# Three groups of stores issued from ScalarE's queue in place of GpSimd's, in a one-core decoder layer

## The chip, the cores and the metric

The kernel runs on one core of one Trainium2 chip. The metric is the device time of one execution in microseconds (us), as the median of the runs shown. Engines are named as in the profile: PE (TensorE matmul), PEld (its weight loads), DVE (VectorE), ACT (ScalarE), POOL (GpSimd), SP (SyncE, which here only issues transfers). A store or a load is issued by the queue of one of these engines and then carried out by the core's 16 DMA engines.

## The reference

One layer over a sequence of 1024 tokens with 1024 channels in float32: four token mixers behind one combined projection, an output projection, a LayerNorm on the residual, then a SwiGLU channel mixer of width 2816 and a second LayerNorm.

```python
h = x * (1 + sc1) + sh1
z = h @ w_in + b_in                       # split into seven groups of 256 channels
y = concat([y_a, y_b, y_c, y_d])          # short conv, pooling, conformer conv (31 taps), state space
x = layer_norm(ALPHA * x + (1 + g1) * (y @ w_o), ln1_g, ln1_b)
h = x * (1 + sc2) + sh2
f = (silu(h @ w_gate) * (h @ w_up)) @ w_down
x = layer_norm(ALPHA * x + (1 + g2) * f, ln2_g, ln2_b)
```

## The kernel before

**Products.** Every large product is done in three passes (`passes`, L130 to L132): each float32 operand is split into a high part, cast by ACT (L80), and the rest, subtracted by DVE (L81). A weight tile is therefore usable when its L80 and its L81 are done; the first matmul that needs the L81 part is the third, L132.

**Halves.** The tokens go in two halves `c` of 512 (`CH`). Half 0 passes the output projection and the first LayerNorm around 255 to 305 us of the span, half 1 around 372 to 460 us.

**The first LayerNorm** works on tiles of 128 tokens, four in a half. `res1` (DVE, L570 and L571) forms the row `r`, `norm_stats` takes its mean and variance (DVE, L500 and L503) and the reciprocal root in ten tiny instructions on POOL (`rsqrt`, L397 to L415, then `lnb` at L578). ACT normalises `r` (L580). The first store keeps it in DRAM as `x1_d` (L581). PE transposes `r` (L588), ACT scales the turned row (L598, eight pieces) into a buffer `tmp`, both parts are split off, and the second store keeps the turned row as `h2_d` (L603). In half 1, DVE subtracts two loaded blocks from it (L609), POOL stores the difference (`t1_d`, L613), and ACT and DVE cast the results into `tb`.

**The gate and up products** of a pair of 128-column blocks `j` (`c11`): `gu_pairs` loads and splits two weight tiles, `c11_mm` computes one block product, ACT keeps a copy of it in `p1` (L643) before PE adds the second one on top, and `c11_act` stores `p1` in DRAM (`p1_d`, L646, the third store of the change), applies SiLU (ACT, L648), multiplies (DVE, L649) and stores the result (`act_d`, L650, POOL). `c11` of the pairs 0 and 1 is interleaved with the LayerNorm of half 0; pairs 2 to 6 run between the halves, beside the 31-tap convolution of half 1 on DVE (L429, "taps") and the conformer norm that follows the taps (`conformer`); later pairs run beside the LayerNorm of half 1. From about 514 us on, seven-product blocks (`strassen`) and the down projection fill PE.

**Order.** PE's order is fixed by hand throughout (`in_order`), and in the stage with the LayerNorm of half 0 the orders of DVE and ACT too. Elsewhere a scheduler sets DVE's, ACT's, POOL's and SP's order from its own estimates when the program is built, so an edit on one queue can move instructions on others. Each engine works through its list strictly in order. Weight loads, all `raw` tiles (four buffers, `p1` among them) and the loads that read the stores back are on SP's queue.

Of the kernel before, what the change touches and what calls it, by code (L numbers as in the profile page):

```python
# [16 lines left out]
P = 128  # L17
# [3 lines left out]
CH = 512  # L21
# [29 lines left out]
def trunk(ctx: ExitStack, tc: tile.TileContext, A, out):  # L51
    nc = tc.nc
    V, S, G, PE, SP = nc.vector, nc.scalar, nc.gpsimd, nc.tensor, nc.sync
# [11 lines left out]
    def mm():  # L65
        return ps.tile([P, 512], F32, name="mm", tag="mm", bufs=6)
# [9 lines left out]
    def tmp(cols=1024):  # L76
        return sl.tile([P, cols], F32, name="tmp", tag="tmp", bufs=3)

    def split(hi, lo, src):
        S.copy(hi, src)  # L80
        V.tensor_tensor(out=lo, in0=src, in1=hi.bitcast(F32), op=SUB)  # L81
# [136 lines left out]
    for i in range(4):  # L218
        r = slice((i % 2) * 64, (i % 2) * 64 + 64)
# [128 lines left out]
    for i in range(2):  # L348
        for hf in range(2):
            w = 2 << (2 * i + hf)  # L350
            r = slice(64 * hf, 64 * hf + 64)
# [133 lines left out]
    x1_d = dr.tile([T // P, P, D], F32, name="x1_d")  # L485
    h2_d = dr.tile([KT, P, T], F32, name="h2_d")
    t1_d = dr.tile([KT // 2, P, CH], F32, name="t1_d")
    p1_d = dr.tile([FT // 2, P, 2, CH], F32, name="p1_d")
# [3 lines left out]
    def norm_stats(r, res=None):  # L492

        st = cst.tile([P, 2, 6], F32, name="lst", bufs=2)
        mv = cst.tile([P, 2], F32, name="lmv", bufs=2)
        rs = cst.tile([P, 1], F32, name="lrs", bufs=2)
        for h in range(2):
            if res:
                run(res, 1)
            V.bn_stats(st[:, h], r[:, h * 512:(h + 1) * 512])  # L500
            if res and h == 0:
                yield
        V.bn_aggr(mv, st)  # L503
        rsqrt(rs, mv[:, 1:2])
        return rs, mv[:, 0:1]
# [68 lines left out]
    def ln1(c, t, r, h2):  # L574

        rs, nm = yield from norm_stats(r)
        nb = cst.tile([P, 1], F32, name="lnb", bufs=2)
        G.tensor_scalar(out=nb, in0=nm, scalar1=rs, scalar2=-1.0, op0=MUL, op1=MUL)  # L578
        yield
        S.activation(r, r, AF.Identity, scale=rs, bias=nb)  # L580
        G.dma_start(x1_d[c * 4 + t], r)  # L581
        yield
        tp = []
        for h in range(2):
            o = mm()
            for k in range(4):
                kk = 4 * h + k
                PE.transpose(o[:, k * P:(k + 1) * P], r[:, kk * P:(kk + 1) * P], ident)  # L588
            tp.append(o)
        yield  # L590
        ht = tmp()
        hv = ht.rearrange("p (k t) -> p k t", k=KT)
        tt = slice(t * P, (t + 1) * P)
        for h in range(2):
            for k in range(4):
                kk = 4 * h + k
                src, dst = tp[h][:, k * P:(k + 1) * P], ht[:, kk * P:(kk + 1) * P]
                S.activation(dst, src, AF.Identity, scale=hA[:, kk:kk + 1], bias=hB[:, kk:kk + 1])  # L598
            if c == 0:
                ks = slice(4 * h, 4 * h + 4)  # L600
                split(h2[:, ks, 0, tt], h2[:, ks, 1, tt], hv[:, ks])
                yield
        G.dma_start(h2_d[:, :, c * CH + t * P:c * CH + (t + 1) * P].rearrange("k p t -> p k t"), hv)  # L603
        if c == 1:

            b11 = raw_p.tile([P, 1024], F32, name="raw", tag="raw", bufs=4)
            bv = b11[:, :CH].rearrange("p (k t) -> p k t", k=4)
            SP.dma_start(bv, h2_d[:4, :, t * P:(t + 1) * P].rearrange("k p t -> p k t"))
            V.tensor_tensor(out=bv, in0=hv[:, :4], in1=bv, op=SUB)  # L609
            split(tb[0][:, :4, 0, tt], tb[0][:, :4, 1, tt], bv)  # L610
            split(tb[1][:, :, 0, tt], tb[1][:, :, 1, tt], hv[:, 5:])
            split(tb[0][:, 4, 0, tt], tb[0][:, 4, 1, tt], hv[:, 4])
            G.dma_start(t1_d[:, :, tt].rearrange("k p t -> p k t"), bv)  # L613
# [29 lines left out]
                S.copy(p1[:, i * CH + lo:i * CH + lo + n], z[i][:, hs])  # L643

    def c11_act(j, z, p1):
        G.dma_start(p1_d[j].rearrange("p a t -> p (a t)"), p1)  # L646
        g = tmp()
        S.activation(g[:, :CH], z[0], AF.Silu)  # L648
        V.tensor_tensor(out=g[:, :CH], in0=g[:, :CH], in1=z[1], op=MUL)  # L649
        G.dma_start(act_d[2 * j][:, :CH], g[:, :CH])  # L650

    def p1_tile():
        return raw_p.tile([P, 1024], F32, name="p1", tag="raw", bufs=4)

    def c11(j, tiles=(None, None)):

        w = gu_pairs(j, tiles)
        yield
        z, p1 = [mm(), mm()], p1_tile()
        c11_mm(w, z, p1, 0)  # L660
        yield
        c11_mm(w, z, p1, 1)
        c11_act(j, z, p1)
# [204 lines left out]
    with in_order(ON_PE):  # L868
# [53 lines left out]
        def stats(t):  # L922
            rr.append(res1(0, t, o0))
            ln.append(ln1(0, t, rr[t], h2))
            run(ln[t], 1)
# [3 lines left out]
    with in_order(ON_PE, ON_DVE, ON_ACT):  # L929
# [16 lines left out]
        wg.append(pair(raw(A["w_up"][0])))  # L946
        run(ln[2], 1)
        ln.append(ln1(0, 3, rr[3], h2))
        run(ln[3], 1)
        B["11"] = [(h2[:, k, 0], h2[:, k, 1]) for k in range(4)]  # L950
        B["21"] = [(h2[:, k, 0], h2[:, k, 1]) for k in range(4, 8)]
        z, p1 = [mm(), mm()], p1_tile()
# [13 lines left out]
        for q in range(2):  # L966
            c11_mm(w1, z1, p11, q, 256, 256)
        c11_act(0, z, p1)
        c11_act(1, z1, p11)
    ln_end = [[i for i in nc.cur_bb.bb.instructions if i.engine == e][-3]  # L970
              for e in (ON_DVE, ON_ACT)]
    fins = []
    with tc.issue_after(ln_end[0]), tc.issue_after(ln_end[1]), in_order(ON_PE):
# [19 lines left out]
        def done(t, o):  # L993
            rr.append(res1(1, t, o))
            ln.append(ln1(1, t, rr[t], None))
            run(ln[t], 1)
# [429 lines left out]
```

## Time and profile before

| | before |
|---|---|
| runs, us | 1037.73, 1038.14, 1041.8 |
| median, us | 1038.14 |
| the profiled execution's own time, us | 1037.87 |
| its span (first to last instruction), us | 1036.1 |
| PE busy, share of the span | 95% |
| DVE, ACT, POOL busy | 71%, 33%, 18% |

The profile is of one execution: 1.8 us of its time lie outside the span. Times of day in the text are us from the span's start. PE's matmuls overlap, so a row's length is longer than its step in the stream.

### The profile page before, as it was taken

The numbers are of one execution on the slowest core, as the hardware profiler recorded it, in microseconds if no ns is written. First come the engines' busy times: TensorE is split into PE (matmuls) and PEld (weight loads), VectorE is DVE, ScalarE is ACT, GpSimd is POOL, SyncE is SP. The second block draws the span as 40 slices with busy tenths as digits, with TensorE's granted clock in tenths as the row PEclk, the third lists the DMA queues.
The fourth block names the chain that finished last, engine by engine and source line by source line (L and its number), as shares of the span: only waits on it lengthen the run. The fifth ranks groups of instructions, "written<-read, shape, count | busy, mean of one in ns | idle before, by whom it ended". The sixth has DMA issues, their size and how long they took to land.

```text
span 1036.1 us, 12527 instructions
## 1 busy us (share of the span) xinstructions
PE 980.8 (95%) x4480; PEld 799.9 (77%) x4480; DVE 737.7 (71%) x1184; ACT 344.5 (33%) x537; POOL 184.4 (18%) x515
## 2 busy tenths in 40 slices
PE   8949999898989989899899999999999999999995
PEld 7837777676887868687688888887888888888884
DVE  5858998888669952757898777776568433776656
ACT  4632211424464351374322222222233333312500
POOL 7990000300351020541000000000000000050013
PEclk9979999998999999899999999999999999999998
DMA  8833212686454363597954344443247534654601
GB/s 314 321 112 104 53 41 90 219 225 223 158 204 172 147 237 104 188 316 267 347 175 159 138 147 152 146 148 111 82 149 284 174 136 142 232 185 148 228 21 61
DMA packets 65694, 177.75 MB, mean 172 GB/s; under 512 B 11040, under 2 KB 17216, under 8 KB 65632
## 3 DMA queue, kind: packets, MB, share of 16 engines
q1 hardware_dynamic: 57760, 149.17, 42.7%
q0 software_dynamic: 7872, 27.79, 6.7%
q8 instruction: 35, 0.57, 0.2%
q14 instruction: 27, 0.22, 0.1%
HBM read 142.26 MB, written 34.09 MB: 170 GB/s over the span
## 4 chain that ended last, share of the span: by engine, by line
PE 60%; DVE 10%; DMA 5%; POOL 4%; ACT 3%; issue 2%; SPq 0%; DVEq 0%; POOLq 0%; ACTq 0%
PE mm L132 18%; PE mm L130 18%; PE mm L131 17%; PE sm L130 2%; PE sm L132 2%; PE sm L131 2%; DMA raw<-in_w_ada_dram 2%; DMA raw<-h_d 2%; DVE pr L81 1%; DVE acc L429 1%; DMA raw<-in_w_gate_dram 1%; DVE raw L168 1%; ACT tmp L598 1%; DVE lst L500 1%; POOL rs_a L397 1%
## 5 line engine op out<-in xcount | busy, mean ns | idle before, releaser
L81 DVE TENSOR_TENSOR pr<-raw,pr 128x1024 fp32r<-128x1024 f32 (+1 forms) x139 | 138.1, 1003 | 77.7 <-ACT pr L80 77.4
L80 ACT CAST pr<-raw 128x1024 fp32r<-128x1024 f32 (+1 forms) x139 | 119.2, 878 | 179.4 <-PE sm L132 68.4
L130 PE MATMUL mm<-bop,pr 128*128 128x512 f32 x264 | 103.2, 391 | 4.2 <-DVE c L767 3.5
L131 PE MATMUL mm<-bop,pr 128*128 128x512 f32 x264 | 102.8, 389 | 0.0
L132 PE MATMUL mm<-bop,pr 128*128 128x512 f32 x264 | 102.7, 389 | 0.0
L130 PE MATMUL mm<-h,pr 128*128 128x512 f32 (+1 forms) x208 | 77.0, 370 | 8.0 <-ACT p L643 7.1
L429 DVE SCALAR_TENSOR_TENSOR acc<-up,pack,acc 128x512 f32<-128x512 f32 x120 | 84.3, 742 | 0.1
L130 PE MATMUL mm<-pr,acts 128*128 128x512 f32 x216 | 84.0, 389 | 0.0
L131 PE MATMUL mm<-pr,acts 128*128 128x512 f32 x216 | 84.0, 389 | 0.0
L132 PE MATMUL mm<-pr,acts 128*128 128x512 f32 x216 | 84.0, 389 | 0.0
L132 PE MATMUL mm<-h,pr 128*128 128x512 f32 (+1 forms) x208 | 75.4, 362 | 2.9 <-DVE pr L81 2.9
L131 PE MATMUL mm<-h,pr 128*128 128x512 f32 (+1 forms) x208 | 75.2, 361 | 0.0
L132 PE MATMUL mm<-tb,pr 128*128 128x512 f32 x176 | 68.8, 391 | 1.1 <-DVE pr L81 1.0
L130 PE MATMUL mm<-tb,pr 128*128 128x512 f32 x176 | 68.7, 390 | 1.0 <-ACT pr L80 1.0
L131 PE MATMUL mm<-tb,pr 128*128 128x512 f32 x176 | 68.5, 389 | 0.0
L397 POOL TENSOR_SCALAR rs_a<-lmv 128x1 f32<-128x1 f32 x16 | 11.0, 689 | 318.1 <-DVE lmv L503 317.8
L168 DVE SCALAR_TENSOR_TENSOR raw<-raw,cond 128x1024 f32<-128x1024 f32 x48 | 58.1, 1218 | 13.3 <-DMA raw<-in_w_ada_dram 13.2
L80 ACT CAST pr<-room 128x512 fp32r<-128x512 f32 x60 | 34.3, 619 | 87.9 <-PE mm L132 83.9
L130 PEld LDWEIGHTS mm<-bop,pr 128*128 128x128 f32 x264 | 49.6, 188 | 16.4 <-DVE c L767 2.9
L132 PEld LDWEIGHTS mm<-bop,pr 128*128 128x128 f32 x264 | 49.6, 188 | 10.3
L131 PEld LDWEIGHTS mm<-bop,pr 128*128 128x128 f32 x264 | 49.6, 188 | 10.1
L131 PE MATMUL mm<-h_a,pr 128*128 128x512 f32 x104 | 42.7, 410 | 13.7 <-DVE h_a L81 13.5
(311 smaller groups left out, 2182.4 us busy)
## 6 DMA issues: line engine op xcount, KB each, us to landing
raw<-in_w_ada_dram SPq DMA_DIRECT2D x48, 512.0 KB, 4.8
raw<-in_w_down_dram SPq DMA_DIRECT2D x44, 512.0 KB, 3.7
raw<-in_w_gate_dram SPq DMA_DIRECT2D x23, 512.0 KB, 4.7
raw<-in_w_up_dram SPq DMA_DIRECT2D x23, 512.0 KB, 4.2
raw<-act_d SPq DMA_DIRECT2D x44, 256.0 KB, 3.3
raw<-in_w_o_dram SPq DMA_DIRECT2D x16, 512.0 KB, 4.4
p_d<-p POOLq DMA_DIRECT2D x11, 512.0 KB, 2.9
act_d<-tmp POOLq DMA_DIRECT2D x11, 512.0 KB, 2.9
```

Source lines behind the costliest of these rows:

```text
L80: S.copy(hi, src)
L81: V.tensor_tensor(out=lo, in0=src, in1=hi.bitcast(F32), op=SUB)
L130: PE.matmul(o, wh, xh, start=first, stop=False, skip_group_check=True)
L131: PE.matmul(o, wh, xl, start=False, stop=False, skip_group_check=True)
L132: PE.matmul(o, wl, xh, start=False, stop=last, skip_group_check=True)
L168: V.scalar_tensor_tensor(out=w, in0=w, scalar=1.0, in1=cond, op0=MUL, op1=MUL, accum_out=mod[:, j:j + 1])
L397: G.tensor_scalar(out=a, in0=v, scalar1=EPS, scalar2=None, op0=ADD)
L429: V.scalar_tensor_tensor(out=o, in0=u, scalar=dww[:, i, j:j + 1], in1=o, op0=MUL, op1=ADD)
L500: V.bn_stats(st[:, h], r[:, h * 512:(h + 1) * 512])
L598: S.activation(dst, src, AF.Identity, scale=hA[:, kk:kk + 1], bias=hB[:, kk:kk + 1])
```

## The change

Three DMA issues move from POOL's list (`G`) to ACT's (`S`). What they store, and where to, is as before.

```diff
@@ ln1
         S.activation(r, r, AF.Identity, scale=rs, bias=nb)
-        G.dma_start(x1_d[c * 4 + t], r)
+        S.dma_start(x1_d[c * 4 + t], r)
@@ ln1
-        G.dma_start(h2_d[:, :, c * CH + t * P:c * CH + (t + 1) * P].rearrange("k p t -> p k t"), hv)
+        S.dma_start(h2_d[:, :, c * CH + t * P:c * CH + (t + 1) * P].rearrange("k p t -> p k t"), hv)
@@ c11_act
-        G.dma_start(p1_d[j].rearrange("p a t -> p (a t)"), p1)
+        S.dma_start(p1_d[j].rearrange("p a t -> p (a t)"), p1)
```

Each of the eight LayerNorm tiles has one of the first and one of the second kind, each of the eleven pairs `j` one of the third: 27 stores. PE's list is the same before and after. The lists of the other engines differ at more places than the three lines; three of them follow (- before, + now).

On POOL, between the reciprocal roots of the first and the second tile of half 1 (`r_3530` is the first tile's row, `lmv` and `lrs` are a tile's variance and reciprocal root):

```order
 L415 TENSOR_TENSOR lrs<-lrs,rs_b_3541 128x1
 L578 TENSOR_SCALAR lnb<-lmv,lrs 128x1
-L581 DMA x_d<-r_3530 128x1024
 L397 TENSOR_SCALAR rs_a_3578<-lmv 128x1
 L398 TENSOR_SCALAR lrs<-rs_a_3578 128x1
```

The store that stood between the two chains is gone from POOL; the second chain now follows the first directly.

On DVE, right after the last tile of half 0 (`h` is the split turned row, `acc` the convolution's sums, `pr<-raw` the low parts of the two weight tiles of pair 2):

```order
 L81 TENSOR_TENSOR h_2321<-tmp,h_2321 128x4x128 x4
-L429 SCALAR_TENSOR_TENSOR acc<-up,pack_471,acc 128x512 x15
-L649 TENSOR_TENSOR tmp<-tmp,mm 128x512 x2
+L429 SCALAR_TENSOR_TENSOR acc<-up,pack_471,acc 128x512 x17
+L649 TENSOR_TENSOR tmp<-tmp,mm 128x512
+L429 SCALAR_TENSOR_TENSOR acc<-up,pack_471,acc 128x512 x3
+L649 TENSOR_TENSOR tmp<-tmp,mm 128x512
 L81 TENSOR_TENSOR pr<-raw,pr 128x1024 x2
```

Twenty taps now stand ahead of the two weight splits of pair 2, where fifteen stood.

On ACT, from the SiLU of pair 7 to the turned row of the third tile of half 1 (`r_3606` is that tile's row), first before:

```order
L648 ACTIVATE tmp<-mm 128x512
L80 CAST tb<-raw 128x4x128
L580 ACTIVATE r_3606<-r_3606,lnb,lrs 128x1024
L80 CAST pr<-raw 128x1024
L598 ACTIVATE tmp<-mm,hB,hA 128x128 x8
L80 CAST tb<-raw 128x4x128
L80 CAST tb<-tmp 128x3x128
L80 CAST tb<-tmp 128x128
L80 CAST pr<-raw 128x1024
L643 COPY p_3813<-mm 128x512 x2
L598 ACTIVATE tmp<-mm,hB,hA 128x128 x8
```

and the same stretch now:

```order
L648 ACTIVATE tmp<-mm 128x512
L598 ACTIVATE tmp<-mm,hB,hA 128x128 x8
L80 CAST tb<-raw 128x4x128
L603 DMA h_d<-tmp 128x8x128
L80 CAST tb<-tmp 128x3x128
L80 CAST tb<-tmp 128x128
L580 ACTIVATE r_3606<-r_3606,lnb,lrs 128x1024
L80 CAST pr<-raw 128x1024
L581 DMA x_d<-r_3606 128x1024
L80 CAST pr<-raw 128x1024
L643 COPY p_3813<-mm 128x512 x2
L598 ACTIVATE tmp<-mm,hB,hA 128x128 x8
```

The third tile's L580 now comes behind the second tile's turned row and its casts, and both weight casts come ahead of the copies L643.

## Rows read from the trace of the kernel before

**Rows 1.** Page, busy time: share of the span and instructions of each engine.

```profile
PE 980.8 (95%) x4480; PEld 799.9 (77%) x4480; DVE 737.7 (71%) x1184; ACT 344.5 (33%) x537; POOL 184.4 (18%) x515
```

**Rows 2.** Windows: busy PE, PEld, DVE, ACT, POOL, then granted clock, DMA share, GB/s.

```profile
800.00:825.00 25.00, 25.00 (x112) 20.68 (x111) 12.40 (x14) 8.79 (x11) 0.00 (x0) 1.00 0.50 168
```

**Rows 3.** Single lines, DMA issues: ns min/median/max, first and last start.

```profile
L581 POOL DMA_DIRECT2D x_d<-r x8: 562/584/804, 272.7 to 454.1; - x8
...
L603 POOL DMA_DIRECT2D h_d<-tmp x8: 895/948/1007, 278.2 to 458.2; - x8
...
L750 SPq DMA_DIRECT2D room<-p_d x10: 326/327/454, 502.1 to 731.6; - x10
...
L674 SPq DMA_DIRECT2D raw<-h_d x16: 319/424/502, 470.5 to 496.7; - x16
```

**Rows 4.** Timeline of ACT, fourth tile of half 0: start, length, [idle before <-releaser].

```profile
298.15 1.24 ACT L580 ACTIVATE r<-r,lnb,lrs 128x1024 f32<-128x1024 f32 x1
...
300.13 1.51 ACT L598 ACTIVATE tmp<-mm,hB,hA 128x128 f32<-128x128 f32 x4 [0.21 <-PE mm L588]
```

**Rows 5.** Timeline of DVE after the fourth tile of half 0.

```profile
305.00 10.02 DVE L429 SCALAR_TENSOR_TENSOR acc<-up,pack,acc 128x512 f32<-128x512 f32 x15
314.94 1.28 DVE L649 TENSOR_TENSOR tmp<-tmp,mm 128x512 f32<-128x512 f32 x2
316.13 2.35 DVE L81 TENSOR_TENSOR pr<-raw,pr 128x1024 fp32r<-128x1024 f32 x2
```

**Rows 6.** Timeline of PE at the start of pair 2.

```profile
317.40 0.50 PE L132 MATMUL mm<-h,pr 128*128 128x512 f32 x1 [0.83 <-DVE pr L81]
```

**Rows 7.** Windows as in rows 2, after two long waits of PE.

```profile
371.80:378.00 6.20, 6.20 (x27) 5.14 (x28) 2.96 (x3) 4.51 (x7) 0.61 (x1) 1.00 0.43 161
...
433.30:439.20 5.90, 5.90 (x14) 4.64 (x15) 1.58 (x3) 4.22 (x12) 4.68 (x14) 0.51 0.45 183
```

**Rows 8.** Timeline, conformer norm: POOL's first instruction, and PE's next matmul.

```profile
364.48 1.11 POOL L397 TENSOR_SCALAR rs_a<-cmv 128x4 f32<-128x4 f32 x1 [0.88 <-DVE cmv L451]
...
371.81 0.50 PE L130 MATMUL mm<-h,pr 128*128 128x512 f32 x1 [2.90 <-ACT p L643]
```

**Rows 9.** Timeline of POOL, first and second tile of half 1.

```profile
422.69 0.26 POOL L578 TENSOR_SCALAR lnb<-lmv,lrs 128x1 f32<-128x1 f32 x1
424.52 0.62 POOL L581 DMA_DIRECT2D x_d<-r  x1 [1.58 <-ACT r L580]
425.23 0.22 POOL L397 TENSOR_SCALAR rs_a<-lmv 128x1 f32<-128x1 f32 x1
...
426.55 2.26 POOL L409 TENSOR_SCALAR rs_b<-rs_c,rs_b 128x1 f32<-128x1 f32 x1
...
431.23 0.26 POOL L578 TENSOR_SCALAR lnb<-lmv,lrs 128x1 f32<-128x1 f32 x1
```

**Rows 10.** Timeline of DVE beside it.

```profile
422.75 0.20 DVE L503 BATCH_NORM_AGGREGATE lmv<-lst 128x2 f32<-128x12 f32 x1
...
423.42 1.22 DVE L571 SCALAR_TENSOR_TENSOR r<-raw,r 128x1024 f32<-128x1024 f32 x1
...
426.35 1.21 DVE L571 SCALAR_TENSOR_TENSOR r<-raw,r 128x1024 f32<-128x1024 f32 x1
...
427.59 1.17 DVE L81 TENSOR_TENSOR pr<-raw,pr 128x1024 fp32r<-128x1024 f32 x1
```

**Rows 11.** Timeline of ACT, second to fourth tile of half 1.

```profile
431.53 1.24 ACT L580 ACTIVATE r<-r,lnb,lrs 128x1024 f32<-128x1024 f32 x1 [5.41 <-POOL lnb L578]
...
433.62 2.91 ACT L598 ACTIVATE tmp<-mm,hB,hA 128x128 f32<-128x128 f32 x8
...
452.48 1.30 ACT L580 ACTIVATE r<-r,lnb,lrs 128x1024 f32<-128x1024 f32 x1
```

**Rows 12.** Timeline of PE, pair 7 and the fourth tile's transposes.

```profile
433.29 0.79 PE L130 MATMUL mm<-h,pr 128*128 128x512 f32 x1 [4.19 <-ACT p L643]
...
454.25 1.03 PE L588 MATMUL mm<-ident,r 128*128 128x128 f32 x8
```

## The prediction

> **What bounds the kernel now.** The first view is the busy table: PE is busy for 95% of the span, DVE for 71%, ACT for 33%, POOL for 18% [rows 1]. So the end is set by PE's stream and by the few places where it waits. The windows over the late part come next: between 800 and 825 us PE is busy for all 25 us at a granted clock of 1.00 [rows 2], and that is the picture nearly throughout from 514 us on. A store issued there from one queue or another has nothing to give, unless it makes PE wait anew. What is left is 260 to 514 us, where both LayerNorms run. PE's timeline there, read for its marks of idle time, gives the waits that count: 0.83 us at 317.40, for a low part from DVE [rows 6]; 2.90 us at 371.81 [rows 8]; 4.19 us at 433.29 [rows 12]. The last two name ACT's copy L643. ACT's own timeline shows that it stood behind L580, which waited 5.41 us for POOL [rows 11]. POOL's timeline gives the reason: the store of the first tile's row, waiting for L580 of that tile and then issuing until 425.14, stood ahead of the second tile's reciprocal root, whose variance DVE had ready at 422.95 [rows 9, 10]. So the stores on POOL do hold something up, once.
>
> **The price of an issue on ACT.** Before, ACT issues nothing here, so no row has it. The nearest rows are SP's issues of the same shapes, 0.33 us for a 128x1024 row and 0.42 us for a turned row; POOL's own are 0.58 and 0.95 us [rows 3]. The bounds are nothing (the issue runs beside the operation ahead of it) and 0.95 us. I take 0.45 us, near SP's larger one, since ACT must also reach the end of L580 or L598 before the store goes out, where the next operation need not.
>
> **A, half 0, 298 to 305 us.** ACT is without idle time ahead of the fourth tile's L580, and L598 right behind waited only 0.21 us for PE [rows 4]. Two issues of the third tile now stand ahead of that L580, the fourth tile's row store between it and L598: 2 x 0.45 + (0.45 - 0.21) = 1.1 us later, bounds 0 and 2.6 (three at 0.95, less the 0.21). DVE's taps then start at 306.1 instead of 305.00 [rows 5].
>
> **B, pair 2.** DVE now has twenty taps ahead of the two splits L81 where it had fifteen. Fifteen took 10.02 us, one 0.67 us [rows 5]; five are 3.35 us. The first split, which now ends near 317.3, ends near 321.75, and PE's third matmul of pair 2 waits until then instead of 317.40 [rows 6]: 1.1 + 3.35 = 4.45 us, no cover left, since PE waits there already. The other operands of pair 2 come from ACT's L80 and are late by A alone.
>
> **C, pairs 2 to 5.** Two things can follow. After the 2.90 us wait PE kept the clock 1.00, with 27 matmuls in 6.20 us; after the 4.19 us wait it was granted 0.51, with 14 matmuls in 5.90 us [rows 7], where 14 x 0.23 = 3.2 would have done: 2.7 us lost. The new wait at pair 2 is as long, in two pieces. If the clock stays up, DVE is late again: its second split of pair 2 ends near 322.9, thirteen taps (8.7), L332 (0.4) and pair 3's first split (1.15) follow, to 333.15, while PE's 48 matmuls of pair 2 (10.9 us) bring it there at 332.65: 0.5 us late. Between that split and pair 4's first stand another split, eight taps and seven operations of about 0.6 us, as L649 [rows 5]: 1.15 + 5.35 + 4.2 + 1.15 = 11.85 us against PE's 10.9, so 0.9 us more, 1.4 in all. If the clock falls, PE is late enough for DVE. I take 2.0, between 1.4 and 2.7; the low bound is 0, if neither comes.
>
> **D, the conformer.** POOL's first step there, L397, lasted 1.11 us, from 364.48 [rows 8], while DVE's timeline has a split L81 running. Only the arrangement of splits around it changes: two of them come before the statistics, one behind. I give 0.9 us back there, bounds 0 and 1.2. The wait of 2.90 us does not soak up the shift, since the chain ahead of it starts from PE's own transposes and shifts with them.
>
> After A to D PE stands later by 1.1 + 3.35 + 2.0 - 0.9 = 5.55 us.
>
> **E, half 1, 422 to 454 us.** The store gone, POOL's second chain starts at about 423.05 instead of 425.23 [rows 9]. Shifted whole it would end 2.2 us sooner than 431.49. But its steps depend on what DVE runs: L409 lasted 2.26 us, from 426.55, while DVE's two-input operations L571 and L81 ran from 426.35 to 428.76 [rows 9, 10]. Steps that meet nothing last 0.22 to 0.26 us [rows 9]. The earlier chain meets L571 of 423.42 [rows 10] and the later pair at another step; I estimate its end at 428.9, 2.6 us sooner. The wait of 4.19 us at PE then becomes 1.6 us, shorter than the 2.90 that did not lower the clock, so the 2.7 us of half clock go too: -5.3 us. A page agrees with the long steps: the Trainium skill, "SBUF — State Buffer", section "SBUF: two separate sides", says that GpSimd and a VectorE operation with two SBUF inputs take a shared pair of ports in turn, each for a whole instruction. By that rule alone the chain ends at 428.9, by the plain shift at 429.3; the sum would differ by 0.4 us.
>
> Against this stands ACT's new order, five issues between 431 and 452 us [rows 11], and the third tile's L580 behind the second tile's turned row. ACT then is what PE waits for at pair 8 and at the fourth tile's transposes (454.25 now [rows 12]): 5 x 0.45 = 2.2 us back. E is -3.1 us, bounds -5.3 and -5.3 + 5 x 0.95 = -0.5.
>
> **F, 454 to 514 us.** The fourth tile's two issues stand in ACT's chain to the last casts: 2 x 0.45, half of it beside PE's products, +0.5 us (0 to 1.9). Beyond, PE has no wait to lengthen.
>
> **Sum.** 5.55 - 3.1 + 0.5 = +2.95 us on the profiled execution's 1037.87: 1040.8; the median of the runs shown is 0.27 us above that execution, so 1041.0.
>
> **The rivals.** *Dear issues (slower).* ACT pays what POOL paid, 0.95 us. For: POOL's two prices for these very stores [rows 3]. Against: SP's. A is 2.6, B 3.35, C 2.0, D -0.9, E -0.5, F 1.9: +8.4, so 1046.5 by the median. It decides from 0.7 us an issue: nine issues on the path, each 0.25 dearer, add 2.25 to 1041.0, which is the bound of half a per cent. Chance 0.25.
> *Free issues (faster).* An issue costs ACT nothing and only the POOL chain's gain is left, with pair 2's delay absorbed, because DVE's later work has fewer taps and catches up before 372. E is -5.3; 1037.87 - 5.3 gives 1032.6. For: the five taps done early are not done later. Against: PE's timeline shows no wait between 318 and 371 us in which it could catch up. It decides if the two L81 end before 318.5. Chance 0.12.
> *No net change.* Issues near 0.1 us, the clock not dropping, DVE in time at pairs 3 and 4: A 0.3, B 3.35, C 0, D -0.9, E -4.8, F 0.1: -2.0, so 1036. Chance 0.18. A rule points the same way: the Trainium skill, "Trainium Kernel Development and Optimization", section "Key Constraints", says that transfers from the SP, ACT and POOL queues share the same 16 DMA engines and that issuing from several saves only issue time; by it nothing lands sooner, and no reader here waits for a landing (the first read back of a turned row is near 470 us, the last such store at 458 [rows 3]).
>
> **How the numbers follow.** My own case has 0.45. About 0.5% (5.2 us) is what a measurement of this kernel tells from no change; that is 1032.9 to 1043.3. The likeliest is 1041.0, its own range 1038 to 1044, so mostly inside that bound. The range reaches down to the rival without net change and up near the dear issues: 1035 to 1046. Faster takes most of the free-issue case, 0.10; slower takes the dear issues, and the top of my own case, 0.31; the rest, 0.59, is the same.
>
> **What would show it.** After the change: ACT's issue rows near 0.45 us; a wait of PE for DVE's L81 of pair 2 near 321.75; the granted clock of the next 6 us (near 0.5, or 1.00 with a shorter second wait at pair 3); the wait ahead of pair 7's first matmul, 1.6 us in place of 4.19, at clock 1.00; the second tile's chain on POOL starting right behind the first's; PE waiting for ACT at the third and fourth tiles of half 1. I am wrong if DVE waits less ahead of pair 2 than the taps say, if PE's clock behaves otherwise after these waits, or if the weight loads on SP, which in the program's lists share completion semaphores with ACT's stores now, begin to wait for them.

## The result, and the profile after

The changed kernel takes 1045.98 us (median of four runs, 1045.38 to 1046.7), the kernel before 1038.07 (four runs, the three of the table and one more): a ratio of 1.0066, with a 95% interval of 1.0046 to 1.0086. It is slower by 0.66%, beyond the half per cent that the prediction took as its bound. The profiled execution took 1045.76 us, its span is 1043.6 us against 1036.1. Of these 7.5 us PE is busy for 5.2 (its list is the same, its mean granted clock 0.975 for 0.980) and idle for 2.3; the busy times of DVE and ACT are what they were, POOL's has lost its issues. Executions of one kernel spread widely (28 of the kernel before, on one chip, took 1034.93 to 1044.23 us at a mean granted clock of 0.972 to 0.982), so a sum read from one pair of profiles holds some chance.

The page of the changed kernel, busy time (as [rows 1]):

```profile
PE 986.0 (94%) x4480; PEld 804.0 (77%) x4480; DVE 737.3 (71%) x1184; ACT 344.8 (33%) x537; POOL 165.7 (16%) x488
```

The single lines of the three stores, now on ACT's queue, as [rows 3] (each from the view of its own line):

```profile
L581 ACTq DMA_DIRECT2D x_d<-r x8: 326/326/348, 270.3 to 456.2; - x8
...
L603 ACTq DMA_DIRECT2D h_d<-tmp x8: 377/377/379, 275.7 to 460.1; - x8
...
L646 ACTq DMA_DIRECT2D p_d<-p x11: 326/327/553, 310.6 to 491.7; - x11
```

An issue mostly lasts 0.33 to 0.38 us on ACT, as long as on SP. The same 14.16 MB go out in 11056 packets on ACT's queue, where POOL's had 3888; the median time from issue to landing is 3.4, 3.3 and 3.4 us for the three groups, where it was 3.5, 3.7 and 2.9. What an issue costs the engine shows in ACT's timeline from the third to the fourth tile of half 0 (to be read beside [rows 4]):

```profile
289.30 0.33 ACTq L581 DMA_DIRECT2D x_d<-r  x1
289.68 0.65 ACT L643 COPY p<-mm 128x256 f32<-128x256 f32 x2 [0.40 <-ACT r L580]
...
296.04 0.62 ACT L80 CAST h<-tmp 128x512 fp32r<-128x512 f32 x1
296.05 0.38 ACTq L603 DMA_DIRECT2D h_d<-tmp  x1
296.57 1.24 ACT L580 ACTIVATE r<-r,lnb,lrs 128x1024 f32<-128x1024 f32 x1
297.83 0.33 ACTq L581 DMA_DIRECT2D x_d<-r  x1
298.20 0.65 ACT L643 COPY p<-mm 128x256 f32<-128x256 f32 x2 [0.40 <-ACT r L580]
```

The store of the turned row needs the eight L598, which are done, so it goes out while the cast L80 runs, and L580 behind it starts without a wait. The store of the normalised row needs the L580 right ahead of it; it can only go out when that has ended (297.81), and the next operation L643 starts 0.40 us late; the third tile's store of that kind does the same (289.30, 289.68). So an issue is free where it has a finished operation to wait for and another one to run beside, and costs 0.40 us where it stores what the engine has just made.

DVE's timeline at pair 2 (as [rows 5]):

```profile
303.61 11.35 DVE L429 SCALAR_TENSOR_TENSOR acc<-up,pack,acc 128x512 f32<-128x512 f32 x17
314.87 0.69 DVE L649 TENSOR_TENSOR tmp<-tmp,mm 128x512 f32<-128x512 f32 x1
315.47 2.07 DVE L429 SCALAR_TENSOR_TENSOR acc<-up,pack,acc 128x512 f32<-128x512 f32 x3
317.45 0.68 DVE L649 TENSOR_TENSOR tmp<-tmp,mm 128x512 f32<-128x512 f32 x1
318.05 2.36 DVE L81 TENSOR_TENSOR pr<-raw,pr 128x1024 fp32r<-128x1024 f32 x2
```

PE's timeline, the waits that the account below rests on (as [rows 6, 8, 12]):

```profile
319.33 0.80 PE L132 MATMUL mm<-h,pr 128*128 128x512 f32 x1 [4.31 <-DVE pr L81]
...
374.55 0.50 PE L130 MATMUL mm<-h,pr 128*128 128x512 f32 x1 [1.66 <-ACT p L643]
...
433.63 0.50 PE L130 MATMUL mm<-h,pr 128*128 128x512 f32 x1 [1.87 <-ACT p L643]
...
448.70 0.50 PE L130 MATMUL mm<-h,pr 128*128 128x512 f32 x1 [2.13 <-ACT p L643]
...
456.27 1.09 PE L588 MATMUL mm<-ident,r 128*128 128x128 f32 x8 [0.25 <-ACT r L580]
...
470.35 0.50 PE L132 MATMUL mm<-tb,pr 128*128 128x512 f32 x1 [1.59 <-DVE pr L81]
...
475.28 0.51 PE L130 MATMUL mm<-tb,pr 128*128 128x512 f32 x1 [2.36 <-ACT pr L80]
```

Windows behind four of these waits (columns as in [rows 2]; as [rows 7]):

```profile
319.30:323.00 3.70, 3.67 (x9) 2.90 (x10) 3.70 (x6) 0.00 (x0) 0.00 (x0) 0.50 0.64 213
433.60:439.50 5.90, 5.87 (x27) 4.86 (x28) 2.43 (x7) 5.01 (x13) 4.68 (x14) 1.00 0.85 291
448.70:453.00 4.30, 4.30 (x12) 3.40 (x13) 0.72 (x1) 3.23 (x9) 0.00 (x0) 0.60 0.64 209
476.00:480.00 4.00, 4.00 (x12) 3.17 (x12) 3.42 (x4) 0.00 (x0) 0.00 (x0) 0.58 0.53 145
```

PE's list is the same in both kernels, so the same matmul can be compared: how much later it starts after than before is PE's shift. It is -2.1 us at 250 us and still at 280 (281.75 before, 279.60 after), for reasons ahead of the change, whose first store goes out at 270.3: the start of a run differs by a microsecond or two. At the fourth tile's transposes of half 0 it is -1.6 (299.44, 297.86). From there it goes to +1.9 at pair 2's third matmul (317.40, 319.33), +3.9 in pair 4 (339.52, 343.45), +2.7 behind the conformer (371.81, 374.55), +0.3 at pair 7 and -2.3 some 25 matmuls later (439.00, 436.70, where before was at half clock), +2.0 at the fourth tile's transposes (454.25, 456.27), +6.1 at 520 us (513.83, 519.97) and +7.5 at the end of the span. Counted from -2.1, the part behind the first moved store is thus 9.6 us in this pair of profiles, gained and lost in several places.

POOL's timeline, second tile of half 1 (as [rows 9]; everything stands 2.64 us later than there, as the 425.33 beside 422.69 shows):

```profile
425.33 0.26 POOL L578 TENSOR_SCALAR lnb<-lmv,lrs 128x1 f32<-128x1 f32 x1
425.70 0.23 POOL L397 TENSOR_SCALAR rs_a<-lmv 128x1 f32<-128x1 f32 x1
...
428.95 1.31 POOL L414 TENSOR_SCALAR rs_b<-rs_b 128x1 f32<-128x1 f32 x1
430.34 1.12 POOL L415 TENSOR_TENSOR lrs<-lrs,rs_b 128x1 f32<-128x1 f32 x1
431.57 0.26 POOL L578 TENSOR_SCALAR lnb<-lmv,lrs 128x1 f32<-128x1 f32 x1
```

The second chain follows the first at once and ends at 431.83, that is 429.2 on the clock of before, 2.3 us sooner. That is the main gain of the change (the other is 1.2 us at the conformer), and PE's wait ahead of pair 7 shows it: 1.87 us in place of 4.19, in this execution at clock 1.00 behind it in place of 0.51.

Where half 1 then loses it again, in three timelines, ACT first:

```profile
444.95 1.04 ACT L80 CAST pr<-raw 128x1024 fp32r<-128x1024 f32 x1
...
447.12 1.04 ACT L80 CAST pr<-raw 128x1024 fp32r<-128x1024 f32 x1 [1.13 <-DMA raw<-in_w_up_dram]
...
453.84 0.62 ACT L80 CAST tb<-raw 128x512 fp32r<-128x512 f32 x1 [1.91 <-DVE raw L609]
```

SP, the loads for pair 8 and for the third and fourth tile:

```profile
442.59 0.35 SPq L73 DMA_DIRECT2D raw<-in_w_up_dram  x1
449.38 0.99 SPq L608 DMA_DIRECT2D raw<-h_d  x2
```

DVE, the third tile's subtraction:

```profile
453.11 0.69 DVE L609 TENSOR_TENSOR raw<-tmp,raw 128x512 f32<-128x512 f32 x1 [3.70 <-DMA raw<-h_d]
```

Pair 8's first weight cast stands at 444.95, behind L598, three `tb` casts and L580. So the splits L81 of pair 8's weights come late (446.02 and 448.19), and with them the `raw` buffers that they read. The third tile's load of the turned row (L608) waits for such a split and is issued only at 449.38; DVE waits 3.70 us for the load, ACT's next cast waits 1.91 us for DVE, and the fourth tile's L580 stands behind that cast.

### The profile page after: what moved, and what is told of

The parts are those of the page before. It is cut to its first block, busy times and chain, and to the rows that moved or that the text cites. A ratio compares the mean times of both kernels' runs of the same rounds, so it can differ in the third digit from the quotient of the medians.

```text
span 1043.6 us, 12514 instructions
## 1 busy us (share of the span) xinstructions
PE 986.0 (94%) x4480; PEld 804.0 (77%) x4480; DVE 737.3 (71%) x1184; ACT 344.8 (33%) x537; POOL 165.7 (16%) x488
## 3 DMA queue, kind: packets, MB, share of 16 engines
q10 hardware_dynamic: 11056, 14.16, 3.7%
## 4 chain that ended last, share of the span: by engine, by line
PE 56%; DVE 9%; DMA 7%; issue 6%; POOL 4%; ACT 3%; SPq 0%; ACTq 0%; DVEq 0%; POOLq 0%
PE mm L132 17%; PE mm L130 17%; PE mm L131 16%; PE sm L132 2%; PE sm L130 2%; PE sm L131 2%; DVE acc L429 2%; DMA raw<-in_w_up_dram 1%; DMA raw<-act_d 1%; DVE raw L168 1%; DMA raw<-in_w_ada_dram 1%; DMA p_d<-p 1%; DVE pr L81 1%; ACT pr L80 1%; DMA raw<-h_d 1%
## 5 line engine op out<-in xcount | busy, mean ns | idle before, releaser
L81 DVE TENSOR_TENSOR pr<-raw,pr 128x1024 fp32r<-128x1024 f32 (+1 forms) x139 | 138.2, 1005 | 82.2 <-ACT pr L80 82.0
L80 ACT CAST pr<-raw 128x1024 fp32r<-128x1024 f32 (+1 forms) x139 | 119.5, 877 | 179.2 <-PE sm L132 61.7
L80 ACT CAST pr<-room 128x512 fp32r<-128x512 f32 x60 | 34.3, 619 | 87.4 <-PE mm L132 83.6
L397 POOL TENSOR_SCALAR rs_a<-lmv 128x1 f32<-128x1 f32 x16 | 10.9, 684 | 322.4 <-DVE lmv L503 322.1
```

The lines of the kernel that those rows point to most:

```text
L397: G.tensor_scalar(out=a, in0=v, scalar1=EPS, scalar2=None, op0=ADD)
```

## The experiments

Theory A, formed from these profiles: the time is lost by the order that the scheduler gave DVE and ACT once the stores had moved, not by the stores being on ACT. Rival B: the issues on ACT, and the waits between stores and loads that now share one kind of queue, cost it. The two are told apart by crossing them. A helper adds order-only edges to the program, along a table of instruction names (they are the same in both kernels):

```diff
+    held_order(nc.cur_bb.bb.instructions, order)
...
+def held_order(seen, order):
+    made = {i.name: i for i in seen}
+    for row in ORDER:
+        names = [f"I-{n}" for n in row.split()]
+        for a, b in zip(names, names[1:]):
+            order(made[b], a)
```

`ORDER` has a row for each engine, from its first to its last difference between the two kernels (DVE 182 instructions, ACT 133, POOL 16, SP 8, the three stores left out). In the first crossed version three instructions of DVE and one of ACT, beyond 490 us, still fall otherwise than in the kernel before; in the second, DVE and ACT have the change's order throughout. All ratios are to the kernel before, run on the same chip, with 95% intervals; an expectation in microseconds is to be read against the 1038.07 above, since the median of before was 1039.14 to 1040.52 in these runs.

**The change's queues, the order of before.** The diff above, applied to the change, with before's rows.

> All 27 stores on ACT as in the change, with the order of DVE, ACT, POOL and SP held to that of before in the stretch where the two differ (the stores themselves aside). Theory A (the loss is one of order: the issues cost ACT little, and the new order of the other instructions makes PE wait): fifteen taps stand ahead of pair 2's splits again, so the 4.31 us wait and the half clock behind it go; POOL's second chain still starts early, so the wait ahead of pair 7 stays under 2 us. I expect 1033 to 1037 us. Theory B (the loss is one of queues: issues on ACT, or waits between stores and loads, cost the time): 1043 to 1047 us, about the change's own time.

Measured: 0.9976 (0.9958 to 0.9995). PE's timeline:

```profile
316.70 0.50 PE L132 MATMUL mm<-h,pr 128*128 128x512 f32 x1 [1.00 <-DVE pr L81]
...
371.55 0.50 PE L130 MATMUL mm<-h,pr 128*128 128x512 f32 x1 [3.35 <-ACT p L643]
...
432.23 0.50 PE L130 MATMUL mm<-h,pr 128*128 128x512 f32 x1 [1.88 <-ACT p L643]
...
445.62 0.50 PE L130 MATMUL mm<-h,pr 128*128 128x512 f32 x1 [0.44 <-ACT p L643]
```

**The queues of before, the change's order.** The same helper in the kernel before, with the change's rows.

> All 27 stores on POOL as before, with the order of DVE, ACT, POOL and SP held to that of the change. Theory A: the wait of some 4.3 us at pair 2 with half clock behind it is there (+3.5 and +1.7), and with the first tile's store back on POOL the 4 us wait ahead of pair 7 is there too: 1044 to 1051 us. Theory B: the stores are where they were, so 1037 to 1040 us.

Measured: 1.0069 (1.0048 to 1.0090). PE's timeline shows both evils, the long wait at pair 2 and the one ahead of pair 7:

```profile
322.02 0.79 PE L132 MATMUL mm<-h,pr 128*128 128x512 f32 x1 [4.15 <-DVE pr L81]
...
439.23 0.50 PE L130 MATMUL mm<-h,pr 128*128 128x512 f32 x1 [3.92 <-ACT p L643]
```

With either queue the order costs 0.7 to 0.9%; with before's order the stores on ACT gain 0.24%, in the same 11056 packets as in the change. B falls, and A stands.

**Two groups, and the third.** Against the change:

```diff
 # x1_d and h2_d on ACT
-        S.dma_start(p1_d[j].rearrange("p a t -> p (a t)"), p1)
+        G.dma_start(p1_d[j].rearrange("p a t -> p (a t)"), p1)
...
 # p1_d alone on ACT
-        S.dma_start(x1_d[c * 4 + t], r)
+        G.dma_start(x1_d[c * 4 + t], r)
...
-        S.dma_start(h2_d[:, :, c * CH + t * P:c * CH + (t + 1) * P].rearrange("k p t -> p k t"), hv)
+        G.dma_start(h2_d[:, :, c * CH + t * P:c * CH + (t + 1) * P].rearrange("k p t -> p k t"), hv)
```

> Only the stores of the normalised and of the turned rows on ACT, p1's left on POOL; the orders fall out so that fifteen taps stand ahead of pair 2's splits, as before. Theory A: no new wait at pair 2, and the early POOL chain in half 1 gives its 5 us, of which some 2 go to ACT's order there: 1033 to 1037 us. Theory B: 16 of 27 issues moved, so 1042 to 1044 us.

Measured: 1.0009 (0.9986 to 1.0032), a miss of A's number: the wait ahead of pair 7 is 1.88 us, but ACT's order of half 1 is near the change's (the second tile's L598 ahead of pair 8's weight casts), and waits of 1.59 us at 467.78 and 1.89 us at 472.23 take the gain back. The granted clock also fell behind the 1.88 us wait here (0.71 from 433.0 to 438.9).

> Only p1's stores on ACT, the rows' stores left on POOL; twenty taps stand ahead of pair 2's splits, as in the change. Theory A: PE waits over 4 us at pair 2, and nothing is gained ahead of pair 7, where the first tile's store stays on POOL: 1042 to 1047 us. Theory B: 11 of 27 issues moved, so 1040 to 1042 us, with no wait at pair 2 that the order explains.

Measured: 1.0057 (1.0035 to 1.0079). PE's timeline:

```profile
319.54 0.79 PE L132 MATMUL mm<-h,pr 128*128 128x512 f32 x1 [4.14 <-DVE pr L81]
...
435.82 0.79 PE L130 MATMUL mm<-h,pr 128*128 128x512 f32 x1 [4.20 <-ACT p L643]
...
458.01 1.09 PE L588 MATMUL mm<-ident,r 128*128 128x128 f32 x8 [2.47 <-ACT r L580]
```

The eleven stores of `p1`, which nothing gains from, are enough to bring the twenty taps and most of the loss.

**Where the order costs.** The helper on the change, with before's rows up to half 1's LayerNorm only, and from there on only.

> The change, with before's order of DVE and ACT held from pair 2 to the start of half 1's first LayerNorm; from there on the order is the change's own. If the two halves of the loss add up, pair 2's 5.5 us go and the conformer's gain of 1.2 us with them, while half 1 keeps its gain of 5 us at pair 7 and its losses (some 4.3 us up to the fourth tile's transposes, some 4 up to 514 us): 2 to 5 us above before, a ratio of 1.002 to 1.005. If pair 2 were the whole loss (the rival), half 1's own order would not matter: a ratio of 0.996 to 0.999, as with the order held everywhere.

Measured: 1.0029 (1.0008 to 1.0049).

> The change, with before's order of DVE, ACT, POOL and SP held from half 1's first LayerNorm on; pairs 2 to 6 are in the change's own order. If the two halves add up: +5.5 at pair 2, -1.2 at the conformer, and half 1 about 3 to 4 us better than before: 0 to 2 us above before, a ratio of 1.000 to 1.003. If pair 2 were the whole loss: a ratio of 1.006 or more, as for the change.

Measured: 1.0013 (0.9993 to 1.0033). From the change's 1.0066 the first takes 0.37%, the second 0.53%, together 0.90%; both at once took 0.90%. Each of these differences is uncertain by some 0.3%, so the two places add up as far as the intervals tell.

**Which engine's order, in half 1.** Both with before's order held up to half 1, and there for ACT alone, or for DVE, SP and POOL but not ACT.

> As the version with before's order held for pairs 2 to 6, and in half 1 before's order held for ACT alone: the third tile's L580 and the weight cast of pair 8 come ahead of the second tile's eight L598 again. Theory C (ACT's order is what half 1 lost): both the copies L643 of pair 8 and the buffer that the third tile's load takes come in time again, and the ratio to before is 0.996 to 0.999, as with all orders held. Theory D (the orders of DVE and SP are what it lost): 1.002 to 1.005, as with half 1 in the change's order.

Measured: 0.9988 (0.9970 to 1.0005).

> The counterpart: before's order held for pairs 2 to 6, and in half 1 for DVE, SP and POOL but not for ACT. Theory C: PE still waits some 2 us for ACT's copies at pair 8 and for L580 at the fourth tile, DVE's split of pair 8's weights waits for its cast: 1.002 to 1.006. Theory D: 0.996 to 0.999.

Measured: 1.0049 (1.0031 to 1.0068), with PE still waiting at pair 8:

```profile
450.41 0.50 PE L130 MATMUL mm<-h,pr 128*128 128x512 f32 x1 [2.27 <-ACT p L643]
```

So it is ACT's order: with before's, the weight cast stands ahead of L598, and the load of the third tile's block goes out in time. In the version with all orders held, ACT's and SP's timelines have it so:

```profile
438.76 1.04 ACT L80 CAST pr<-raw 128x1024 fp32r<-128x1024 f32 x1
439.70 2.90 ACT L598 ACTIVATE tmp<-mm,hB,hA 128x128 f32<-128x128 f32 x8
```

```profile
439.80 0.34 SPq L73 DMA_DIRECT2D raw<-in_w_up_dram  x1
441.08 5.80 SPq L608 DMA_DIRECT2D raw<-h_d  x2
```

**The price of an issue.** First with fewer of them: the store of the normalised rows (`x1_d`) alone on ACT, 8 issues for 27, before's order held.

> Only the stores of the normalised rows on ACT (8 of 27), the other two groups on POOL, and before's order held as far as the orders of the change and of before differ. If an issue on ACT costs next to nothing, this is as fast as all 27 stores on ACT in the same order: a ratio of 0.996 to 0.999, with the wait ahead of pair 7 near 1.9 us. If each issue on ACT costs 0.4 us of the path or more, the some nine issues on it that are gone bring 2 to 4 us more: a ratio of 0.992 to 0.995.

Measured: 0.9969 (0.9949 to 0.9989), not to be told from the 0.9976 with all 27; the intervals leave room for a difference of up to some 3 us. Then with more of them, each store in two halves, before's order held:

```diff
-        S.dma_start(x1_d[c * 4 + t], r)
+        S.dma_start(x1_d[c * 4 + t][:, :512], r[:, :512]); S.dma_start(x1_d[c * 4 + t][:, 512:], r[:, 512:])
...
-        S.dma_start(p1_d[j].rearrange("p a t -> p (a t)"), p1)
+        for a in range(2): S.dma_start(p1_d[j][:, a], p1[:, a * CH:(a + 1) * CH])
```

(and `h2_d` in two lots of four blocks likewise).

> All 27 stores on ACT with before's order held everywhere, each store cut in two halves: 54 issues on ACT in place of 27, the same bytes. If an issue runs beside the operation ahead of it and costs the path next to nothing, the ratio to before stays within 0.002 of the 0.9976 of the version with whole stores. If an issue costs 0.4 us of the path, the nine or so on it add 4 us: 1.001 or more.

Measured: 1.0021 (1.0005 to 1.0038), what I expected of dear issues and not of cheap ones. ACT's timeline of the halved stores shows a part of it, at the place of the first ACT fence above:

```profile
300.17 1.24 ACT L580 ACTIVATE r<-r,lnb,lrs 128x1024 f32<-128x1024 f32 x1 [0.43 <-issue]
301.44 0.85 ACTq L581 DMA_DIRECT2D x_d<-r  x2
302.33 0.65 ACT L643 COPY p<-mm 128x256 f32<-128x256 f32 x2 [0.92 <-PE mm L588]
```

One issue fits under the cast of 0.62 us, two do not (0.43 us of wait), and L643 now starts 0.92 us late where it was 0.40. The profile names PE's L588 for that wait, but L643 starts where the two issues end (302.29). At this place the price is 0 for a covered issue, 0.4 to 0.5 for each one that is not. That the whole loss is made of such prices is not shown: the halves also go out in more packets (13920 for 11056), and the longest wait that this profile adds, 2.56 us at 472.28, is for the split of a weight whose load came late.

**A better version.** All 27 stores on ACT, the order of before held but left free around the conformer, where the change has the shorter wait:

> All 27 stores on ACT, before's order held for pairs 2 to 5 and from half 1 on, but not around the conformer norm, where the scheduler may choose again. It chooses there what the change has around the reciprocal root (L81 moved off it), which gave PE 1.66 us of wait instead of 2.90: 1 to 1.5 us less than with before's order held everywhere, and no half clock behind that wait: a ratio of 0.994 to 0.998.

Measured: 0.9978 (0.9964 to 0.9991): the conformer's wait is 1.79 us, but a new one of 1.36 us for a split stands at 365.39. Last, the normalised rows' store alone on ACT, before's order, and ACT's two copies L643 of pair 7 (3694, 3707) ahead of the second tile's L580 (3738); of ACT's row in the table only this place differs:

```diff
-3738 3694 3707
+3694 3707 3738
```

> Only the normalised rows' stores on ACT, before's order held, and in ACT's list the two copies L643 of pair 7 ahead of the second tile's L580 in place of behind it. PE's last wait there (1.88 us for L643, which stood behind an L580 that waited 3.11 us for POOL) should go, since the products that the copies read are done by then: 1.5 to 1.9 us less than with the order as it was, a ratio to before near 0.995. If PE then waits as long for L580 at the second tile's transposes, nothing is gained: 0.997.

Measured: 0.9992 (0.9974 to 1.0010), a miss: more than either ratio expected. The 1.88 us wait is gone, and others stand later:

```profile
451.43 1.09 PE L588 MATMUL mm<-ident,r 128*128 128x128 f32 x8 [0.86 <-ACT r L580]
...
468.71 0.50 PE L130 MATMUL mm<-tb,pr 128*128 128x512 f32 x1 [2.38 <-ACT pr L80]
```

At 468.71 ACT had waited for a weight load. It is not shown what made that load late. The best version stays the normalised rows' stores on ACT with before's order, 0.31% faster than before, and not to be told from the other two at 0.9976 and 0.9978.

## Why the prediction was right in parts and low in sum

The measured 1045.98 lies inside the range by 0.02 us, less than its own runs differ by, so that it fell inside is luck; the likeliest 1041.0 was 5 us too low. The change is slower by 0.66%, to which 0.31 was given. The terms below add up to +9.7 us with what was lost beyond 520 us, and the profiled execution had gained 2.1 before the first moved store, which no term holds. The case that came closest in time, dear issues (1046.5), is wrong as a mechanism: an issue lasts 0.33 to 0.38 us, not 0.95.

- **A (+1.1), right in the main.** +0.8: DVE's taps start at 303.61 for 305.00, 1.4 us sooner, where the third tile's L580 started 2.2 sooner (288.03 for 290.19). Of the three issues one is covered by a cast; the third tile's L581 costs 0.40, the fourth's 0.40 less the 0.21 of slack; the other 0.2 is a cast's wait for a weight load.
- **B (+3.35), right.** The shift grows from -1.6 to +1.9; less the 0.2 of A that falls behind the transposes, that is 3.3, five taps.
- **C (+2.0), right in size, wrong as a choice.** I held the two alternatives, half clock or late splits, to exclude each other. Both came: 1.7 us of half clock behind the 4.31 us wait, and 0.3 at the first splits of pair 4.
- **D (-0.9), right.** -1.2; L397 lasts 0.23 us, with no split beside it.
- **E, the gain (-5.3), right in size, half of it by luck.** -5.0 by 436.70. Of this, 2.6 us hung on the clock staying at 1.00 behind the shorter wait, which I took from one wait of 2.90 us; behind the same wait of 1.87 or 1.88 us it fell in six of the nine later versions that have it. The chain ended 2.3 us sooner, nearer to the plain shift (429.3) than to the 428.9 worked out with the ports. The long steps do lie beside two-input operations: L414 and L415 in the POOL fence, while DVE had an L571 from 429.00 and an L81 from 430.24. The Trainium skill, "SBUF — State Buffer", section "SBUF: two separate sides", agrees with this trace as to which steps are long (1.31 and 1.12 us, where the steps that meet nothing last 0.19 to 0.34).
- **E, what ACT gives back (+2.2), the step that failed.** It was +4.3 by the fourth tile's transposes, and its cause was not "5 x 0.45". It was the order that the same part names, "the third tile's L580 behind the second tile's turned row", which I had priced by its issues alone: the two versions that part half 1's orders by engine show that ACT's order loses it, through pair 8's weight casts and a `raw` buffer that comes free late, and the granted clock of 0.60 behind the 2.13 us wait adds some 1.6 us.
- **F (+0.5), the other term that failed.** +4.1 by 520 us: 1.59 and 2.36 us of waits at 470.35 and 475.28 for splits and casts of weights whose loads came late (ACT's cast at 470.34 had waited 3.61 us; the load was issued at 466.08 for 462.82, PE being 2.0 us late), and a granted clock of 0.58 behind them. "Beyond, PE has no wait to lengthen" was wrong. With half 1's order of before held they shrink to one of 0.57 us at 466.56.

Beyond 520 us another 1.4 us is lost, 0.75 of it in a wait of PE for DVE's L778 at 795.64; why DVE was late there is not shown. That issues cost next to nothing (the third rival) holds for those that are covered; that the clock would stay up at pair 2 and nothing else would bind does not. Its remark that no reader waits for a landing is wrong in two ways. L608 reads turned rows of half 0 back from 427.58 us on, long before 470, though 120 us behind their stores. And SP's weight loads did wait for `p1`'s stores to land, 59.2 us in all before (260 to 514 us) and 72.8 in the change. More of such waits was a sign named for being wrong; but it was 82.0 us in the version with the change's queues and before's order, which is faster, so these waits do not set the time. The rule named there, that transfers from several queues save only issue time (the Trainium skill, "Trainium Kernel Development and Optimization", section "Key Constraints"), agrees with the landing times above and with the crossing: with the order held, moving the stores gained 0.24%, and the one gain seen in the trace is that of POOL's issue ahead of the second chain.

## What to carry to other kernels

Where a scheduler sets the order, an edit on one queue is two edits: measure it with the old order held before blaming the queue. Price a moved issue by what stands ahead of it on the new engine: free where what it stores is finished and an operation runs that lasts longer than the issue, a little over the issue's own length where it stores what was just made (0.40 us here). And price a reordering by the buffers that come free later, since the loads behind them are late next.

## What the runs showed of the hardware that I had not expected

The granted clock does not follow the length of the wait ahead alone (1.00 is 2.4 GHz, 0.50 is 1.2; a value between is a stretch with some of each). In the change it fell behind waits of 4.31, 2.13 and 2.36 us (0.50, 0.60 and 0.58 in the windows above) and not behind one of 1.87; before, it did not fall behind one of 2.90 ([rows 7, 8]). Nor does the same wait decide it. Ahead of pair 7 the change and nine of the later versions all wait 1.87 or 1.88 us. The clock stayed at 1.00 in four of the ten, and was 0.71 over the next 5.9 us in the other six. Here are the windows behind this wait, first in the version with the normalised rows' store alone on ACT (1.88 us of wait, at 430.71), then in the version with the change's queues and before's order (432.23 above):

```profile
430.70:436.60 5.90, 5.89 (x19) 4.68 (x20) 1.90 (x6) 5.13 (x14) 4.80 (x13) 0.71 0.85 309
...
432.20:438.10 5.90, 5.87 (x27) 4.85 (x28) 2.14 (x6) 5.48 (x14) 4.69 (x15) 1.00 0.90 292
```

What decides it is not shown. The wait of 2.13 us cost PE 3.7 with the slow stretch behind it, and a shorter wait is no guarantee of full clock.
